# The meta tokens' part of a Mamba-2 scan's states: a product with 16 rows replaced by one with 128

## The chip, the cores and the metric

The kernel runs on one core of a Trainium2 chip. The metric is the device time of one execution in microseconds, lower is better. Three runs of the kernel before took 1002.24, 1003.0 and 1005.76 us; their median, 1003.0 us, is the time before.

TensorE multiplies matrices. An instruction pair does it: a weight load puts a stationary operand (rows x columns) into the array, and a matmul streams a moving operand through it and writes PSUM. The rows are the dimension that is summed over. A float32 product is issued as two passes, so two loads and two matmuls. A transpose is a product of a tile with the identity. VectorE (DVE in the profile), ScalarE (ACT) and GpSimd (POOL) do the rest; SyncE (SP) and GpSimd issue most of the DMAs.

## The reference, cut to what matters

A layer of a hybrid decoder: 512 tokens with 16 learned meta tokens ahead of them, so 528 positions, 1024 channels. One of its branches is a Mamba-2 scan with 32 heads of 64 channels in 8 groups of 4 heads, in chunks of 128 positions. The sequence is padded in front, so that the 16 meta tokens are a chunk of their own. The part that the change touches is the states of the chunks:

```python
a_cs = jnp.cumsum(a_dt, axis=2)
...
decay_states = jnp.exp(a_cs[:, :, -1:] - a_cs)
states = jnp.einsum("bclgn,bclgr,bclgrp->bcgrpn", bf, decay_states, xdt)
```

For each chunk c and group g this is a sum over the chunk's positions l of B (128 state channels n) times x (4 heads x 64 channels), weighted per position and head by dt (it is in xdt = x * dt) and by the decay to the end of the chunk. For the meta tokens' chunk the sum has 16 terms, for the three later chunks whose states are needed 128.

## The kernel before, in words

Everything stands with channels on the partitions and positions in the free dimension. `group_proj` computes for one group the projections and the short convolution: `bt` (B, 128 x 528), `ct` (C, 128 x 512), `xc` (x, two tiles of 128 x 528) and `zt`. Positions 0 to 15 of `bt` and `xc` are the meta tokens; `tok(c)` selects the 128 positions of chunk c behind them. `ssd` does the group's scan. Both are generators: `weave` interleaves the scan of group g with the projections of group g + 1 (in the last group with `out_part`, and in group 4 with `out_half` too). The order on each engine is planned ahead from these; pools give the tiles, and an instruction waits for the last reader of the space that its tile takes.

Before the first group, `dt_out` turns dt and its sums to position-major form: `dtok` and `dtm` (16 x 2 x 32: dt and the cumulated a*dt of the meta tokens), and from them the decays `dec` (for the chunks) and `decm` (16 x 32, for the meta tokens). It runs while the gates' projections (`gate_pool`) and the normalization of u (`norm_u`) go on.

In `ssd`, the first step transposes B and x, so that positions stand on the partitions. Three chunks of B and the 16 meta positions go into one PSUM bank, `ptb` (lines 473 to 475); two ScalarE copies take them to `btok` (128 x 3 x 128, line 476) and `btm` (16 x 128, line 477). The meta positions of x go to `ptm` (line 480) and from there, times dt, to `xdtm` (16 x 256, VectorE, line 481). The four chunks of x go to `ptx` and, times dt, to `xdt` (lines 488 and 489). Two more VectorE multiplies apply the decays: `xddm` from `xdtm` (line 494) and `xdd` from `xdt` (line 495). Lines 499 to 513 make the decay matrix in `abc`.

The second step multiplies C with B into `pcb` (line 522), and then makes the four states in two PSUM banks `pst`: the meta tokens' with 16 rows (line 529), the three chunks' with 128 rows (line 531). In every group the eight loads and matmuls of `pcb`, the two of line 529 and the six of line 531 follow each other directly on TensorE. A ScalarE copy (line 533) takes the first state, and VectorE accumulates the others (lines 538 and 539). The third step makes the outputs `po` and `py` from the states and from `abc` (lines 550 and 556); later steps normalize them to `yh` and `yl` (lines 581 to 585), which `out_half` (products `pso`) and `out_part` (`psp`) read as float32r pairs of a high and a low part.

The scan's tiles come from the pool `gs`, whose space is used by others after the scan: among these the 16 T tiles (`t13h` to `t42l`, line 889), which GpSimd's queue loads in order from device memory.

Of the kernel before, what the change touches and what calls it, by code (L numbers as in the profile page):

```python
# [9 lines left out]
F32 = mybir.dt.float32  # L10
F32R = mybir.dt.float32r
AF = mybir.ActivationFunctionType
ALU = mybir.AluOpType

P = 128
D = 1024
SEQ = 512
NM = 16
# [4 lines left out]
R = 4  # L23
HEADS = 32
# [39 lines left out]
def kernel(ctx: ExitStack, tc, xT, x, w, f1, f2, vec, fnw, out):  # L64
    nc = tc.nc
    act, dve, pe, pool = nc.scalar, nc.vector, nc.tensor, nc.gpsimd

    const = ctx.enter_context(tc.tile_pool(name="const", bufs=1, side="left"))
# [64 lines left out]
    ident = const.tile([P, P], F32, name="ident")  # L133
# [20 lines left out]
    dtm = const.tile([NM, 2, HEADS], F32, name="dtm")  # L154
    dec = const.tile([P, 4, HEADS], F32, name="dec")
    cdec = const.tile([P, 4, HEADS], F32, name="cdec")
    decm = const.tile([NM, HEADS], F32, name="decm")

    u_stack = ExitStack()
    up = u_stack.enter_context(tc.tile_pool(name="up", bufs=1, side="left"))  # L160
# [12 lines left out]
    def psum1(name):  # L173
        return psb.tile([P, 512], F32, tag="s", name=name)
# [40 lines left out]
    H = HEADS  # L215
# [105 lines left out]
    for t, name in ((rsh, "dgh"), (rsl, "dgl")):  # L321
        d = pre.tile([NT, 6, NT], F32R, tag="sq", name=name, bufs=2)
# [3 lines left out]
    for i in range(2):  # L326
        pb = psum1(f"pb1_{i}")
        c = slice(3 * i, 3 * i + 3)
        for n in range(2):
            pe.matmul(pb[:, : 3 * NT], ones_r[:NT], dg[n][:, c, :].rearrange("p a b -> p (a b)"),  # L330
                      start=n == 0, stop=n == 1)
# [11 lines left out]
    for c in range(4):  # L343
        r = slice(c * H, (c + 1) * H)
# [19 lines left out]
    for c in (slice(0, P), slice(P, W)):  # L364
        n = c.stop - c.start
# [4 lines left out]
    def dt_out():  # L370

        pt = psum1("pt_dt")
        for j, src in enumerate((dt, acs)):
            pe.transpose(pt[:, j * P : (j + 1) * P], src[:, :P], ident)
            pe.transpose(pt[:NM, 256 + j * H : 256 + (j + 1) * H], src[:H, P:], ident[:H, :H])
        dve.tensor_copy(dtok.rearrange("p a c h -> p (a c h)"), pt[:, :256])
        dve.tensor_copy(dtm.rearrange("p a h -> p (a h)"), pt[:NM, 256 : 256 + 2 * H])
        pq = psum1("pq_dt")
        pe.matmul(pq[:, :128], sel[:, 0, :], dtok[:, 1, :, :].rearrange("p c h -> p (c h)"),
                  start=True, stop=True)  # L380
        pe.matmul(pq[:NM, 128 : 128 + H], sel[:NM, 1, :NM], dtm[:, 1, :], start=True, stop=True)
        fl = lambda t: t.rearrange("p c h -> p (c h)")
        dve.tensor_tensor(fl(dec), pq[:, :128], fl(dtok[:, 1, :, :]), op=ALU.subtract)
        dve.tensor_tensor(decm, pq[:NM, 128 : 128 + H], dtm[:, 1, :], op=ALU.subtract)
        act.activation(fl(dec), fl(dec), AF.Exp)
        act.activation(decm, decm, AF.Exp)
        act.activation(fl(cdec), pq[:, :128], AF.Exp)


# [65 lines left out]
    def bc(ap, n):  # L455
        return ap.unsqueeze(len(ap.shape)).to_broadcast(list(ap.shape) + [n])

    def ssd(g, cur):

        xc, bt, ct, zt = cur  # L460
        hs = slice(R * g, R * g + R)
        tok = lambda c: slice(NM + c * P, NM + (c + 1) * P)
        ctok = lambda c: slice(c * P, (c + 1) * P)
        flat = lambda t: t.rearrange("p r d -> p (r d)")
# [1 line left out]
        abc_load[g] = nc.gpsimd.dma_start(abc, acs_d[hs, :].partition_broadcast(P))  # L466

        xdt = gs.tile([P, 4, R, 64], F32, tag="xdt", name=f"xdt{g}")
        xdtm = gs.tile([NM, R, 64], F32, tag="xdtm", name=f"xdtm{g}")
        btok = gs.tile([P, 3, P], F32, tag="btok", name=f"btok{g}")  # L470
        btm = gs.tile([NM, P], F32, tag="btm", name=f"btm{g}")
        ptb = psum1(f"ptb{g}")
        for c in range(3):
            pe.transpose(ptb[:, c * P : (c + 1) * P], bt[:, tok(c)], ident)
        pe.transpose(ptb[:NM, 3 * P :], bt[:, :NM], ident)
        act.copy(btok.rearrange("p c n -> p (c n)"), ptb[:, : 3 * P])
        b_meta[g] = act.copy(btm, ptb[:NM, 3 * P :])
        pm = psum1(f"ptm{g}")
        for i in range(2):
            pe.transpose(pm[:NM, i * P : (i + 1) * P], xc[:, i, :NM], ident)  # L480
        dve.tensor_tensor(xdtm, pm[:NM, :256].rearrange("p (r d) -> p r d", r=R),
                          bc(dtm[:, 0, hs], 64), op=ALU.mult)
        for b in range(2):
            pt = psum1(f"ptx{g}_{b}")
            for c in range(2):
# [4 lines left out]
                              pt.rearrange("p (c r d) -> p c r d", c=2, r=R),  # L490
                              bc(dtok[:, 0, 2 * b : 2 * b + 2, hs], 64), op=ALU.mult)
        xdd = gs.tile([P, 3, R, 64], F32, tag="xdd", name=f"xdd{g}")
        xddm = gs.tile([NM, R, 64], F32, tag="xddm", name=f"xddm{g}")
        dve.tensor_tensor(xddm, xdtm, bc(decm[:, hs], 64), op=ALU.mult)
        x_decayed[g] = dve.tensor_tensor(xdd, xdt[:, :3, :, :], bc(dec[:, :3, hs], 64), op=ALU.mult)

        eb = gs.tile([P, 2, SEQ], F32, tag="eb", name=f"eb{g}")
# [28 lines left out]
        st = [gs.tile([P, R, 64], F32, tag=f"st{c}", name=f"st{c}_{g}") for c in range(4)]  # L526
        pss = [psum1(f"pst{g}_{b}") for b in range(2)]
        pv = [pss[c // 2][:, (c % 2) * 256 : (c % 2) * 256 + 256] for c in range(4)]
        pe.matmul(pv[0], btm, flat(xddm), start=True, stop=True)
        for c in range(3):  # L530
            pe.matmul(pv[c + 1], btok[:, c, :], xdd[:, c, :, :].rearrange("p r d -> p (r d)"),
                      start=True, stop=True)
# [7 lines left out]
        for rs_ in ((slice(0, 2), slice(2, R)) if g == G - 1 else (slice(0, R),)):  # L540
            n = rs_.stop - rs_.start
            masked[g] = dve.tensor_tensor(dm[:, rs_], dm[:, rs_], cbm.unsqueeze(1).to_broadcast([P, n, 4, P]),
                                          op=ALU.mult)
# [3 lines left out]
        for i in range(2):  # L547
# [5 lines left out]
            for c in range(4):  # L553
                for j in range(2):
                    r = 2 * i + j
# [33 lines left out]
    done, abc_load, masked, y_first, squared, b_meta, x_decayed = {}, {}, {}, {}, {}, {}, {}  # L589
# [22 lines left out]
    for d in range(GATES_FIRST):  # L612
        gate_pool(d, True)
        if d == 0:
            dt_out()
# [3 lines left out]
    gs = gc_stack.enter_context(tc.tile_pool(name="gs", bufs=1, side="left", reuse_waits="tile"))  # L619
# [137 lines left out]
    for g in range(G):  # L757
        nxt = group_tiles(g + 1) if g + 1 < G else None
        fill = [group_proj(g + 1, nxt, GATE_AT.get(g))] if nxt else [out_part()]
        if g == 4:  # L760
            fill = [out_half()] + fill
        if g in SUMS_AT:
            fill.append(sums_of_u(SUMS_AT.index(g), g))
        if g in SETS_AT:
            fill.append(weight_sums_at(g))
        weave(ssd(g, cur), fill, 2 if g == 4 else 1)
        cur = nxt
# [633 lines left out]
    for c in range(NC - 1):  # L1401
        z, e = c == 0, c == NC - 2

        n = 2 * c + 3
# [63 lines left out]
    c = NC - 1  # L1468
# [14 lines left out]
    for t in range(4):  # L1483
        T, st = t // 2, slice((t % 2) * P, (t % 2 + 1) * P)
        n = 0
        for half in range(2):
            parts = [(0, 512)] if half == 0 or t < 3 else [(0, 256), (256, 256)]
            for a, m in parts:
# [3 lines left out]
                i = 0  # L1492
# [4 lines left out]
                for k, seg in ((1, (A11, 3)[T]), (0, (A12, A22)[T])):  # L1497
                    wh, wl = wq[k, half]
                    for p in range(2):
                        x0 = p * 512 + a  # L1500
                        f = i == 0 and not (T == 0 and half == 0) and not a
                        i += 1
                        for lhs, rhs in ((hh, wh), (hh, wl), (hl, wh)):
                            pe.matmul(ps, lhs[:, p, seg, st], rhs[:, x0 : x0 + m], start=f and lhs is hh and rhs is wh,
                                      stop=i == 4 and lhs is hl, skip_group_check=True)
# [150 lines left out]
```

## Time and profile before

| | us |
|---|---|
| median of three runs | 1003.0 |
| lowest and highest run | 1002.24, 1005.76 |
| span of the profiled execution | 1001.4 |
| scan of the eight groups, in the profiled execution | 70 to 460 |

The profile is one execution on the chip, taken by the hardware profiler; its own time is its span, 1001.4 us from the first to the last instruction, 1.6 below the median of the runs. Engines: PE is TensorE's matmuls, PEld its weight loads, which overlap the matmuls. A group's line reads: line of the kernel, engine, operation, output<-inputs, shape of output and input, how often | busy time in us, mean ns of one | idle time of the engine just before them, and what ended most of it. "issue" is idle time for which the profile names no other engine. In the timeline a row begins with its start and its duration in us, and rows of equal instructions that follow each other are merged with a count (x3); a shape such as 16*128 is rows times columns of the stationary operand. In the chain of waits, a row is the time that an instruction added to the chain that ended last. Ends of matmuls are modelled.

### The profile page before, as it was taken

Reading aid. Unit: us, or ns where it says so; the run is one execution under the profiler, and the core shown is the slowest. Engines: PE = TensorE matmul, PEld = TensorE weight load, DVE = VectorE, ACT = ScalarE, POOL = GpSimd, SP = SyncE. Lnnn points to the kernel's source line nnn. Section 1 sums busy time; section 2 is a strip of 40 time slices with the busy share of each in tenths; the row PEclk is TensorE's granted clock in tenths of the full one; section 3 lists DMA queues with packets and bytes.
Section 4 is the critical chain, followed back from the end, with each engine's and each line's share of the span. In section 5 each row is a group of like instructions: output and inputs, shape, how many; then the busy total and the mean of one; then the engine's idle time right before and its main releaser. Section 6 shows DMA issues by size and latency. Waiting matters only on the chain.

```text
span 1001.4 us, 15539 instructions
## 1 busy us (share of the span) xinstructions
PE 993.2 (99%) x6095; PEld 878.3 (88%) x6095; DVE 793.2 (79%) x1147; ACT 602.8 (60%) x840; POOL 88.1 (9%) x148
## 2 busy tenths in 40 slices
PE   9999999999999999999999999999999999999997
PEld 7889898999889998988998888888889999999986
DVE  7988797979736687979789667876988888888885
ACT  8675958595827439483255343368666656656654
POOL 0022101111002011002201001121100000000000
PEclk9999999999999999999999999999999999999999
DMA  7378763678238635417978632879654464454432
GB/s 242 92 281 226 202 185 117 193 188 234 63 104 253 164 99 160 132 38 213 280 203 234 230 105 71 238 194 303 182 189 148 149 189 149 146 187 150 127 105 85
DMA packets 56202, 171.47 MB, mean 171 GB/s; under 512 B 6400, under 2 KB 7744, under 8 KB 55104
## 3 DMA queue, kind: packets, MB, share of 16 engines
q1 hardware_dynamic: 36576, 105.86, 32.5%
q0 software_dynamic: 18832, 63.71, 24.3%
q8 instruction: 48, 0.79, 0.3%
q10 hardware_dynamic: 720, 0.91, 0.3%
q14 instruction: 26, 0.21, 0.1%
HBM read 161.90 MB, written 48.40 MB: 210 GB/s over the span
## 4 chain that ended last, share of the span: by engine, by line
PE 98%; DMA 1%; ACT 0%; DVE 0%; issue 0%; SPq 0%; ACTq 0%
PE px L191 12%; PE px L1291 8%; PE alpha L1359 6%; PE pz L191 6%; PE px L193 6%; PE px L1294 4%; PE alpha L1362 3%; PE pgp L191 3%; PE pz L193 3%; PE pgs L191 3%; PE py L556 2%; PE pso L127 2%; PE po L550 2%; PE wo_alpha L1053 1%; PE pso L128 1%; PE pso L130 1%
## 5 line engine op out<-in xcount | busy, mean ns | idle before, releaser
L93 ACT CAST whi<-raw 128x1024 fp32r<-128x1024 f32 (+2 forms) x98 | 98.5, 1014 | 105.7 <-PE px L193 33.2
L95 DVE TENSOR_TENSOR wlo<-raw,whi 128x1024 fp32r<-128x1024 f32 (+2 forms) x98 | 114.7, 1176 | 50.9 <-ACT whi L93 33.1
L191 PE MATMUL px<-uh,whi 128*128 128x264 f32 (+1 forms) x448 | 113.2, 291 | 0.0
L193 PE MATMUL px<-ul,whi 128*128 128x264 f32 (+1 forms) x448 | 110.5, 285 | 0.0
L191 PEld LDWEIGHTS px<-uh,whi 128*128 128x128 f32 x448 | 84.6, 189 | 1.8 <-issue 1.4
L193 PEld LDWEIGHTS px<-ul,whi 128*128 128x128 f32 x448 | 84.3, 188 | 0.4 <-issue 0.2
L1066 DVE TENSOR_TENSOR ht<-ht,alpha 128x1024 f32<-128x1024 f32 x35 | 42.7, 1219 | 29.1 <-PE alpha L1359 29.1
L989 ACT CAST shi<-rawf 128x1024 fp32r<-128x1024 f32 x42 | 44.2, 1051 | 28.7 <-PE alpha L1362 18.2
L191 PE MATMUL px<-uh,wlo 128*128 128x264 f32 (+1 forms) x448 | 58.5, 283 | 0.0
L191 PEld LDWEIGHTS px<-uh,wlo 128*128 128x128 f32 x448 | 55.9, 188 | 0.0
L1359 PE MATMUL alpha<-shi,hh 128*128 128x512 f32 x140 | 55.2, 394 | 0.0
L1362 PE MATMUL alpha<-shi,hl 128*128 128x512 f32 x140 | 54.7, 391 | 0.0
L990 DVE TENSOR_TENSOR slo<-rawf,shi 128x1024 fp32r<-128x1024 f32 x42 | 51.2, 1218 | 0.6 <-ACT shi L989 0.6
L1294 PE MATMUL px<-vsl,shi 128*128 128x256 f32 x192 | 47.4, 280 | 0.0
L1291 PE MATMUL px<-vsh,shi 128*128 128x256 f32 x192 | 47.4, 281 | 0.0
L193 PE MATMUL pz<-ul,whi 128*128 128x512 f32 x112 | 43.6, 390 | 0.0
L191 PE MATMUL pz<-uh,whi 128*128 128x512 f32 x112 | 43.6, 389 | 0.0
L577 DVE RECIPROCAL rs<-rs 128x128 f32<-128x128 f32 x32 | 27.2, 909 | 13.9 <-ACT rs L575 13.8
L1359 PE MATMUL alpha<-slo,hh 128*128 128x512 f32 x140 | 37.4, 389 | 0.0
L1291 PEld LDWEIGHTS px<-vsh,shi 128*128 128x128 f32 x192 | 36.2, 188 | 0.9
L1294 PEld LDWEIGHTS px<-vsl,shi 128*128 128x128 f32 x192 | 36.1, 188 | 0.9
L1294 PE MATMUL px<-vl,shi 128*128 128x256 f32 x144 | 36.1, 283 | 0.0
(558 smaller groups left out, 2859.1 us busy)
## 6 DMA issues: line engine op xcount, KB each, us to landing
raw<-in_w SPq DMA_DIRECT2D x104, 512.0 KB, 4.4
f_t<-in_f POOLq DMA_DIRECT2D x38, 512.0 KB, 6.7
f_s<-in_f POOLq DMA_DIRECT2D x26, 512.0 KB, 8.6
b<-in_f SPq DMA_DIRECT2D x21, 512.0 KB, 4.6
rawf<-in_f SPq DMA_DIRECT2D x36, 256.0 KB, 3.2
rawf<-f_t SPq DMA_DIRECT2D x36, 256.0 KB, 3.0
abc<-acs_d POOLq DMA_DIRECT2D x8, 1024.0 KB, 7.6
f_t<-f_t POOLq DMA_DIRECT2D x12, 512.0 KB, 4.4
```

The costliest lines, as they stand in the source:

```text
L93: act.copy(hi[:, c], raw[:, c])
L95: dve.tensor_tensor(lo[:, c], raw[:, c], hi[:, c].bitcast(F32), op=ALU.subtract)
L191: pe.matmul(o, wt, rhs[0][k][:, c], start=part == 0 and k == 0, stop=part == 1 and k == NK - 1)
L193: pe.matmul(o, wt, rhs[1][k][:, c], start=False, stop=False)
L577: dve.reciprocal(rs[:, ctok(c)], rs[:, ctok(c)])
L989: splits.append((act.copy(hi, src), dve.tensor_tensor(lo, src, hi.bitcast(F32), op=ALU.subtract)))
L990: dve.tensor_tensor(lo, src, hi.bitcast(F32), op=ALU.subtract)))
L1066: added[0] = dve.tensor_tensor(o, o, src, op=op)
L1291: pe.matmul(ps, m, f[k][0], start=start and not low and k == 0, stop=stop and low == 1 and k == 3, skip_group_check=True)
L1294: pe.matmul(ps, m, f[k][1], start=False, stop=False, skip_group_check=True)
L1359: pe.matmul(ps[t], hh[:, p, seg, st], m, start=bool(first and not low and p == 0), stop=bool(last and low and p == 1), skip_group_check=True)
L1362: pe.matmul(ps[t], hl[:, p, seg, st], m, start=False, stop=False, skip_group_check=True)
```

## The change

The meta tokens' chunk is treated as a whole chunk of 128 positions: positions 0 to 127, of which the first 16 are the meta tokens. The 112 others get weight zero.

- `wmeta` (128 x 32) takes the place of `decm` (16 x 32). It is set to zero once at the start. `dt_out` writes its first 16 rows: the decay, as before, and then times dt (one multiply more, once).
- The transposes of lines 475 and 480 take positions 0 to 127 instead of 0 to 15: 8 + 16 transposes with 128 stationary columns instead of 16.
- `btok` has four parts and is copied by one ScalarE instruction of 512 columns; `btm` and its copy are gone.
- `xddm` (128 x 256) is made by one VectorE multiply with `wmeta`, from PSUM; `xdtm` and its multiply are gone.
- The first state's product has 128 rows. Rows 16 to 127 add zeros, so the state is the same sum.

A partition's share of the pool `gs` becomes 1 KB smaller (`xdtm` 1 KB and `btm` 0.5 KB go, `btok` grows by 0.5 KB), so the tiles behind lie at other places. The later lines of the changed kernel have numbers that are lower by up to two.

```diff
-    decm = const.tile([NM, HEADS], F32, name="decm")
+    wmeta = const.tile([P, HEADS], F32, name="wmeta")
+    dve.memset(wmeta, 0.0)
...
-        dve.tensor_tensor(decm, pq[:NM, 128 : 128 + H], dtm[:, 1, :], op=ALU.subtract)
+        dve.tensor_tensor(wmeta[:NM], pq[:NM, 128 : 128 + H], dtm[:, 1, :], op=ALU.subtract)
         act.activation(fl(dec), fl(dec), AF.Exp)
-        act.activation(decm, decm, AF.Exp)
+        act.activation(wmeta[:NM], wmeta[:NM], AF.Exp)
+        dve.tensor_tensor(wmeta[:NM], wmeta[:NM], dtm[:, 0, :], op=ALU.mult)
         act.activation(fl(cdec), pq[:, :128], AF.Exp)
...
-        xdtm = gs.tile([NM, R, 64], F32, tag="xdtm", name=f"xdtm{g}")
-        btok = gs.tile([P, 3, P], F32, tag="btok", name=f"btok{g}")
-        btm = gs.tile([NM, P], F32, tag="btm", name=f"btm{g}")
+        btok = gs.tile([P, 4, P], F32, tag="btok", name=f"btok{g}")
+        xddm = gs.tile([P, R, 64], F32, tag="xddm", name=f"xddm{g}")
         ptb = psum1(f"ptb{g}")
         for c in range(3):
             pe.transpose(ptb[:, c * P : (c + 1) * P], bt[:, tok(c)], ident)
-        pe.transpose(ptb[:NM, 3 * P :], bt[:, :NM], ident)
-        act.copy(btok.rearrange("p c n -> p (c n)"), ptb[:, : 3 * P])
-        b_meta[g] = act.copy(btm, ptb[:NM, 3 * P :])
+        pe.transpose(ptb[:, 3 * P :], bt[:, :P], ident)
+        b_meta[g] = act.copy(btok.rearrange("p c n -> p (c n)"), ptb)
         pm = psum1(f"ptm{g}")
         for i in range(2):
-            pe.transpose(pm[:NM, i * P : (i + 1) * P], xc[:, i, :NM], ident)
-        dve.tensor_tensor(xdtm, pm[:NM, :256].rearrange("p (r d) -> p r d", r=R),
-                          bc(dtm[:, 0, hs], 64), op=ALU.mult)
+            pe.transpose(pm[:, i * P : (i + 1) * P], xc[:, i, :P], ident)
+        dve.tensor_tensor(xddm, pm[:, :256].rearrange("p (r d) -> p r d", r=R),
+                          bc(wmeta[:, hs], 64), op=ALU.mult)
...
-        xddm = gs.tile([NM, R, 64], F32, tag="xddm", name=f"xddm{g}")
-        dve.tensor_tensor(xddm, xdtm, bc(decm[:, hs], 64), op=ALU.mult)
...
-        pe.matmul(pv[0], btm, flat(xddm), start=True, stop=True)
+        pe.matmul(pv[0], btok[:, 3, :], flat(xddm), start=True, stop=True)
```

## The prediction

> **What bounds the kernel now.** I read the head of the page first (span, busy times, chain), then the busy times by stage, then the chain around one of the products that the change rewrites, then TensorE's weight loads there one by one.
>
> ```profile
> span 1001.4 us, 15539 instructions
> PE 993.2 (99%) x6095; PEld 878.3 (88%) x6095; DVE 793.2 (79%) x1147; ACT 602.8 (60%) x840; POOL 88.1 (9%) x148
> ...
> PE 98%; DMA 1%; ACT 0%; DVE 0%; issue 0%; SPq 0%; ACTq 0%
> ```
>
> The chain that ends last runs on TensorE for 98% of the span. VectorE (DVE) and ScalarE (ACT) have spare time. So an edit counts where it takes time out of TensorE's own stream, or makes TensorE wait. The next view gives the stages, and shows which engine is full in each.
>
> ```profile
> core 0: us, PE busy (x) PEld busy (x) DVE busy (x) ACT busy (x) POOL busy (x), PEclk, DMA share, GB/s
> 0.00:70.00 70.00, 67.85 (x426) 58.03 (x427) 59.26 (x109) 50.36 (x75) 9.06 (x22) 1.00 0.59 192
> 70.00:460.00 390.00, 389.98 (x2649) 350.39 (x2648) 299.65 (x470) 255.64 (x342) 43.19 (x70) 1.00 0.56 161
> 460.00:640.00 180.00, 180.00 (x958) 155.89 (x956) 136.19 (x190) 74.19 (x101) 21.67 (x35) 1.00 0.66 200
> 640.00:1001.00 361.00, 355.42 (x2067) 314.00 (x2065) 298.14 (x380) 222.59 (x322) 14.17 (x21) 1.00 0.55 164
> ```
>
> The scan of the eight groups, where the change sits, runs from 70 to 460 us. TensorE is busy in all of it, at the full granted clock. "Busy" is modelled, though: a matmul that is held up is only drawn longer. The chain shows more, because it splits the same stretch by who used it. This is group 0's piece:
>
> ```profile
> 76.54 0.89 PE pcb L522 x8
> 77.43 0.62 PE pst L529 x2
> 78.06 1.49 PE pst L531 x6
> 79.55 0.12 PE px L191
> ```
>
> All eight instructions of pst have 256 columns (a float32 product is issued as two passes). The two with 16 rows (L529) cost 0.31 us each, the six with 128 rows (L531) 0.25 us. The weight loads of the same moment show why:
>
> ```profile
> 76.82 0.42 PEld L522 LDWEIGHTS pcb<-ct,bt 128*128 128x128 f32 x3
> 77.36 0.29 PEld L529 LDWEIGHTS pst<-xddm,btm 16*128 16x128 f32 x2
> 77.98 1.16 PEld L531 LDWEIGHTS pst<-xdd,btok 128*128 128x128 f32 x6 [0.33 <-issue]
> 79.17 0.19 PEld L191 LDWEIGHTS px<-uh,whi 128*128 128x128 f32 x1
> ...
> 78.52 0.62 PEld L531 LDWEIGHTS pst<-xdd,btok 128*128 128x128 f32 x3
> ```
>
> Loads normally follow each other at the pace of the matmuls. The three pcb loads step by (0.42 - 0.19)/2 = 0.115 us, the last three pst loads by (0.62 - 0.19)/2 = 0.215 us. The last pcb load is at 76.82 + 0.23 = 77.05, so the next is due at 77.165; it comes at 77.36. Behind the 16-row pair the load engine sits idle for 0.33 us, and the profile names no other engine ("issue"). So TensorE empties when it goes from 128 rows to 16, and again on the way back.
>
> **The change part by part. The product with 128 rows** (L529). If nothing empties, the first pst load is at 77.165, the second 0.115 later (behind pcb's last matmul), and the next six steps and the one to px take 0.215 each: 77.165 + 0.115 + 7 x 0.215 = 78.785, against 79.17 now. That is 0.385 us, and the chain says the same: 0.62 + 1.49 - 8 x 0.215 = 0.39. The view by line says that this repeats:
>
> ```profile
> L531 PEld LDWEIGHTS pst<-xdd,btok 128*128 128x128 f32 x48 | 8.5, 189 | 3.5 <-issue 2.3 <-DVE wlo L95 0.3
> L529 PEld LDWEIGHTS pst<-xddm,btm 16*128 16x128 f32 x16 | 2.3, 183 | 1.0
> ```
>
> Sixteen loads of L529 are eight groups, and 2.3 + 0.3 us is eight times 0.33. So 8 x 0.385 = 3.1 us go. Bounds: no saving at all if the emptying has another cause; 3.1 if every pair behaves as here. That rows are the cause is supported by a second place, in dt_out, where 128 and 32 rows alternate:
>
> ```profile
> 51.01 0.14 PEld L374 LDWEIGHTS pt_dt<-ident,ddt 128*128 128x128 f32 x1
> 51.43 0.08 PEld L375 LDWEIGHTS pt_dt<-ident,ddt 32*16 32x16 f32 x1 [0.29 <-issue]
> ```
>
> Again an idle 0.29 us named "issue" where the row count falls. I take 3.1.
>
> Two rules bear on it. The Trainium skill, TensorE: Matmul & The Clock Gate (Step-by-step: what each phase is for), says that a weight load's time goes with its columns and that its row count does not matter; the loads agree (183 ns with 16 rows, 189 with 128), and by that alone the product would save nothing. The Trainium skill, TensorEngine Tiling (Array Packing) (Key Properties), says that changing the tiling mode drains the engine; the idle 0.33 us agrees, and by it the saving is the one above.
>
> **Wider transposes** (L475, L480): 8 + 16 of them go from 16 to 128 stationary columns.
>
> ```profile
> 69.25 0.09 PEld L475 LDWEIGHTS ptb<-ident,bt 128*16 128x16 f32 x1
> 69.36 0.20 PEld L480 LDWEIGHTS ptm<-ident,xc 128*16 128x16 f32 x2
> 69.57 0.91 PEld L488 LDWEIGHTS ptx<-ident,xc 128*128 128x128 f32 x8
> ```
>
> A 16-column load lasts 0.09 us. The 128-column ones last about 0.14 (the L374 row), but both start 0.11 us apart (69.25 to 69.36 to 69.57 by three; (0.91 - 0.14)/7 for the eight). The cover is the matmul of the neighbour, which streams the same 128 columns of ident either way. Cost 0; without that cover 24 x 0.05 = 1.2 us, the upper bound.
>
> **VectorE and ScalarE.** Per group one VectorE multiply goes (xddm from xdtm), the other now covers 128 partitions; on ScalarE two copies become one of 512 columns.
>
> ```profile
> L539 DVE TENSOR_TENSOR st<-st,pst 128x256 f32<-128x256 f32 x24 | 9.9, 411 | 0.1
> L481 DVE TENSOR_TENSOR xdtm<-ptm,dtm 16x256 f32<-16x256 f32 x8 | 3.3, 406 | 2.9 <-PE ptm L480 2.9
> L494 DVE TENSOR_TENSOR xddm<-xdtm,decm 16x256 f32<-16x256 f32 x8 | 3.2, 403 | 0.0
> L384 DVE TENSOR_TENSOR decm<-pq_dt,dtm 16x32 f32<-16x32 f32 x1 | 0.2, 169 | 0.0
> ...
> L476 ACT COPY btok<-ptb 128x384 f32<-128x384 f32 x8 | 3.8, 475 | 0.0
> L533 ACT COPY st<-pst 128x256 f32<-128x256 f32 x8 | 2.9, 363 | 1.4 <-PE pst L531 1.4
> L477 ACT COPY btm<-ptb 16x128 f32<-16x128 f32 x8 | 2.0, 250 | 0.0
> ```
>
> On VectorE, 256 columns cost 406 ns on 16 partitions and 411 on 128, so the surviving multiply costs the same, and 8 x 0.403 = 3.2 us go. The new product in dt_out costs one 0.17 us, and the memset under 0.1. On ScalarE, 128 columns more cost 475 - 363 = 112 ns, so a 512-column copy takes some 587 ns (an estimate from these two rows), and 8 x (475 + 250 - 587) = 1.1 us go. None of this is on the chain: I count 0, and keep 0.40 + 0.14 us per group as the bound of a gain. The new product waits for ScalarE's exp, with norm_u's work queued behind it; it lies some 12 us ahead of the scan, at worst 0.2 us.
>
> **Moved instructions.** The planned order of the two kernels differs little. What matters is group 4: on VectorE one slice of L509 and xdd now stand ahead of the pair yl (L585), and TensorE's first pcb stands inside the pso burst.
>
> ```profile
> 260.43 1.27 DVE L489 TENSOR_TENSOR xdt<-ptx,dtok 128x512 f32<-128x512 f32 x2
> 261.63 0.40 DVE L494 TENSOR_TENSOR xddm<-xdtm,decm 16x256 f32<-16x256 f32 x1
> 262.46 1.29 DVE L585 TENSOR_TENSOR yl<-yt,yh 128x512 fp32r<-128x512 f32 x2 [0.43 <-ACT yh L584]
> 263.67 0.95 DVE L495 TENSOR_TENSOR xdd<-xdt,dec 128x768 f32<-128x768 f32 x1
> 264.54 0.67 DVE L509 TENSOR_SCALAR abc<-abc,dtok 128x128 f32<-128x128 f32 x3
> ...
> 263.81 0.19 PEld L128 LDWEIGHTS pso<-yl,whi 128*128 128x128 f32 x1 [0.21 <-DVE yl L585]
> ```
>
> After xdt (261.70) come 0.22 us of L509 and 0.95 of xdd, then yl until 262.87 + 1.29 = 264.16 instead of 263.75. TensorE already waits 0.21 us for the second yl; it would wait 0.4 longer, less the 0.115 of a pcb pass done early: +0.3 us (bounds 0 and 0.4). Behind it on TensorE stand the rest of pso and pst, all in order. In groups 2 and 3 xdd also moves forward, but there no pso burst reads yl at that time.
>
> The T tiles that POOL loads after the scan get their waits at other places, because the scan's tiles lie 1 KB lower. This is their queue and their first use:
>
> ```profile
> 475.46 2.12 POOL L889 DMA_DIRECT2D t42l<-t_d42l  x4
> ...
> DMA to landing us min/median/max: 7.1/8.3/8.7
> ...
> 509.98 0.28 PE L843 MATMUL pxx<-t42h,whiS 128*128 128x260 f32 x1
> ```
>
> The last one is issued at 477.0, lands some 8.7 us later at 486, and is read from 510: 24 us of room, so 0.
>
> **Sum**: 1001.4 - 3.1 + 0 + 0.3 = 998.6 us for the profiled execution. The median of the timed runs, 1003.0, lies 1.6 above that execution's span, so 1003.0 - 2.8 = 1000.2 us. Nothing later takes it back by these rows: from 460 to 640 us TensorE is busy throughout, at 0.66 DMA share.
>
> **The rivals.** *More than the emptying.* If the 0.54 us per group freed on VectorE and ScalarE also shortened a wait of TensorE in each group, 8 x 0.54 = 4.3 us more would go: 995.9. For it: TensorE's loads do wait for VectorE here and there (the 0.21 us above). Against it: VectorE and ScalarE have 0% of the chain.
>
> *Not what it says.* The emptying stays, because something else between pcb and pst makes it (a change of bank or of operands): 1003.0 + 0.3 = 1003.3. For it: the row count leaves the load's duration alone. Against it: the idle time behind the pair and the second place in dt_out. The rule of the Trainium skill on row counts (TensorE: Matmul & The Clock Gate, the section named above) gives this by itself.
>
> *Slower.* The T tiles come too late. POOL issues in order; if an early load now waits for the last reader of a scan tile late in the out_part stretch, all sixteen queue behind it. It decides from 24 us of delay on; at 32 us TensorE would stand for 8 us: 1000.2 + 8 = 1008.2. For it: the waits do move to earlier loads. Against it: the same readers have finished by 475 in the trace, and the issue of sixteen loads takes only 16 x 0.53 = 8.5 us.
>
> **How the numbers follow.** Half a per cent, 5.0 us, is about what a measurement can tell from no change, so faster means under 998.0 and slower over 1008.0. Chances: the forecast 0.62, more than the emptying 0.22, not what it says 0.08, the slower rival 0.08. The forecast alone spans 999 to 1001.5: 0 to 1.2 us of transposes and 0 to 0.4 in group 4 on one side, some of the freed time on the other. The range that leaves out the far half of the second case, most of the third and all of the fourth is 995.5 to 1003.0. Faster: 0.22 and 0.05 from the lower edge of the forecast, 0.27. Slower: 0.08. Within: 0.65.
>
> **What would show it.** Right: no "issue" idle of about 0.33 us ahead of the pst loads, the eight passes from pcb's last load to px in 1.62 us instead of 2.0, the transposes still 0.11 us apart, and a span of about 998.6. Wrong: the idle time stays, or it goes and the span keeps its length (then a wait took its place, in group 4's pso first), or the span shrinks by over 5 us (then VectorE or ScalarE had held TensorE after all).

## The result, and the profile after

| | before | after |
|---|---|---|
| median of 22 runs each, us | 1003.2 | 1001.38 |
| lowest and highest run, us | 1002.24, 1005.76 | 1000.4, 1004.98 |
| span of the profiled execution, us | 1001.4 | 999.8 |

The ratio of the times is 0.9982, with a 95% interval of 0.9976 to 0.9988. So the change saves 1.8 us: a gain that can be told from nothing, but inside the half per cent that the prediction called no change. The forecast was a saving of 2.8 us, to 1000.2, and a span of 998.6 us for the profiled execution; it came to 999.8.

The head of the profile after, and the first line of its chain of waits:

```profile
span 999.8 us, 15519 instructions
PE 991.7 (99%) x6095; PEld 879.2 (88%) x6095; DVE 790.8 (79%) x1141; ACT 602.6 (60%) x832; POOL 88.3 (9%) x148
...
PE 96%; ACT 2%; DMA 0%; issue 0%; DVE 0%; SPq 0%; ACTq 0%
```

TensorE still sets the end, and executes as many instructions as before. ScalarE now has 2% of the chain. Next, TensorE's weight loads in group 0's scan after the change (start, duration, instruction), then the two groups of pst by line:

```profile
76.07 0.98 PEld L520 LDWEIGHTS pcb<-ct,bt 128*128 128x128 f32 x8
76.97 0.30 PEld L527 LDWEIGHTS pst<-xddm,btok 128*128 128x128 f32 x2
77.30 1.27 PEld L529 LDWEIGHTS pst<-xdd,btok 128*128 128x128 f32 x6
78.59 0.19 PEld L192 LDWEIGHTS px<-uh,whi 128*128 128x128 f32 x1
```

```profile
L529 PEld LDWEIGHTS pst<-xdd,btok 128*128 128x128 f32 x48 | 9.1, 190 | 1.2
L527 PEld LDWEIGHTS pst<-xddm,btok 128*128 128x128 f32 x16 | 2.4, 192 | 0.0
```

The idle 0.33 us named "issue" is gone in all groups: of the 3.5 us of idle time ahead of the three-chunk loads 1.2 are left, and none ahead of the meta tokens' pair; what is left is named by no wait. From the first pst load to px it takes 78.59 - 76.97 = 1.62 us. Before, the pair was due at 77.165 and px came at 79.17: 2.005.

To see where a gain goes, one can match the matmuls of two traces in their order, and take the difference of the start times of the same matmul. Where this difference (after less before) jumps, time was won or lost. In after it jumps by -0.387 us at the pst pair of every group, so 8 x 0.387 = 3.10 us were won there. But from 70 to 460 us, over the whole scan, the difference falls by only 2.05 us, and ahead of and behind the scan it moves by -0.19 and +0.58. The experiments look for the missing 1.05 and 0.58.

### The profile page after: what moved, and what is told of

It reads as the page before. It is cut to its first block, busy times and chain, and to the rows that moved or that the text cites. A ratio compares the mean times of both kernels' runs of the same rounds, so it can differ in the third digit from the quotient of the medians.

```text
span 999.8 us, 15519 instructions
## 1 busy us (share of the span) xinstructions
PE 991.7 (99%) x6095; PEld 879.2 (88%) x6095; DVE 790.8 (79%) x1141; ACT 602.6 (60%) x832; POOL 88.3 (9%) x148
## 4 chain that ended last, share of the span: by engine, by line
PE 96%; ACT 2%; DMA 0%; issue 0%; DVE 0%; SPq 0%; ACTq 0%
PE px L192 12%; PE px L1289 8%; PE alpha L1357 6%; PE px L194 6%; PE pz L192 5%; PE px L1292 4%; PE alpha L1360 3%; PE pgs L192 3%; PE pgp L192 3%; PE pz L194 3%; PE py L554 2%; PE po L548 2%; PE pf L128 1%; PE pf L127 1%; PE wo_alpha L1051 1%; PE pgp L194 1%
```

## The experiments

Each kernel is the changed one with the edit shown. Unless said otherwise, its time and ratio are against runs of the kernel before on the same chip at the same time. Four numbers come up for all of them, so they stand together here: the change of TensorE's start times against the trace of before (us, negative is a gain) over the first four groups (70 to 240 us), group 4 with what runs beside it (240 to 310), the last three groups (310 to 460), and the rest (460 to 990). Ahead of the scan, from 0 to 70 us, the executions differ from before's by -0.70 (rows16) to +0.71 us (rows64), all of it in the first 30 us but for 0.13 us in dt_rows and g4_dt; this is left out.

| kernel | median | ratio, 95% interval | 70-240 | 240-310 | 310-460 | rest |
|---|---|---|---|---|---|---|
| after | 1001.38 | 0.9982, 0.9976-0.9988 | -1.09 | -0.01 | -0.94 | +0.58 |
| again | 1001.66 | 0.9989, 0.9980-0.9999 | -1.07 | +0.65 | -0.96 | +0.07 |
| rows16 | 1003.18 | 0.9999, 0.9990-1.0007 | -0.01 | +0.06 | +0.03 | +0.65 |
| rows64 | 1003.89 | 1.0002, 0.9993-1.0010 | +0.12 | +0.05 | -0.20 | +0.44 |
| rows72 | 1000.98 | 0.9975, 0.9965-0.9984 | -1.20 | +0.13 | -1.03 | +0.07 |
| g4_order | 1001.54 | 0.9983, 0.9974-0.9992 | -1.10 | +0.04 | -0.95 | +0.03 |
| dt_rows | 1001.66 | 0.9987, 0.9978-0.9996 | -1.08 | 0.00 | -0.96 | +0.07 |
| g4_dt | 1001.68 | 0.9984, 0.9976-0.9993 | -1.08 | +0.23 | -0.55 | +1.70 |
| g4_acc | 1001.40 | 0.9980, 0.9971-0.9989 | -1.08 | -0.07 | -0.89 | +0.45 |
| g4_dve | 1001.43 | 0.9976, 0.9966-0.9986 | -1.08 | +0.01 | -0.93 | +0.01 |
| rows72_dve | 1000.92 | 0.9974, 0.9965-0.9983 | -1.19 | -0.01 | -1.01 | +0.01 |

By the emptying alone the three stretches of the scan would read -1.55, -0.39 and -1.16.

### How many rows it takes

```diff
-        pe.matmul(pv[0], btok[:, 3, :], flat(xddm), start=True, stop=True)
+        pe.matmul(pv[0], btok[:16, 3, :], flat(xddm)[:16], start=True, stop=True)
```

This is rows16; rows64 and rows72 have 64 and 72 in both places. All else in the change stays: the wide transposes, one copy, one multiply.

> The changed kernel with the first 16 rows alone given to the meta tokens' product (the rows behind are zero, so the sum is the same); wide transposes, one copy of 512 columns, one multiply and the order of all engines stay as in the changed kernel. Theory (the array empties where the row count changes): the idle 0.33 us named issue is back behind the pair in all eight groups, the eight pst passes take 0.387 us longer each time, span 999.8 + 3.1 = 1002.9, so about 1.0011 of the time before. Rival (the gain came from the freed VectorE and ScalarE time): span stays near 999.8, ratio near 0.998. Wide transposes cost 0 if the loads stay 0.11 us apart.

> As rows16, with 64 rows in the product. If the array empties because it goes to a form with fewer row strips (32 or 64) and back, 64 rows cost as much as 16: idle 0.33 us per group, span near 1002.9, ratio about 1.001. If only the smallest form (up to 32 rows) does it, 64 rows are as good as 128: span 999.8, ratio 0.998. If the cost grows with the rows left out, about half: span 1001.3.

> As rows16, with 72 rows in the product. If the forms are 32, 64 and 128 rows, 72 rows run in the form of 128: no idle time behind the pair, span 999.8, ratio 0.998. If any row count other than the neighbour's empties the array: idle 0.33 us per group, span near 1002.9, ratio 1.001. The sums with 88 rows in the prologue (L330) follow their neighbours at the usual 0.12 us in the profile before, which speaks for the first.

The loads of pst by line, first of rows16, then of rows64, then of rows72:

```profile
L529 PEld LDWEIGHTS pst<-xdd,btok 128*128 128x128 f32 x48 | 8.5, 189 | 3.5 <-issue 2.3 <-DVE wlo L95 0.3
L527 PEld LDWEIGHTS pst<-xddm,btok 16*128 16x128 f32 x16 | 2.3, 182 | 1.0
```

```profile
L529 PEld LDWEIGHTS pst<-xdd,btok 128*128 128x128 f32 x48 | 8.5, 189 | 3.5 <-issue 2.3 <-DVE wlo L95 0.3
L527 PEld LDWEIGHTS pst<-xddm,btok 64*128 64x128 f32 x16 | 2.4, 184 | 1.0
```

```profile
L529 PEld LDWEIGHTS pst<-xdd,btok 128*128 128x128 f32 x48 | 9.1, 189 | 1.3
L527 PEld LDWEIGHTS pst<-xddm,btok 72*128 72x128 f32 x16 | 2.4, 191 | 0.0
```

With 16 and with 64 rows the idle time is that of before, to the tenth; with 72 it is that of after. So the rows alone make it, and the step lies between 64 and 72 rows. The time follows: rows16 and rows64 take what the kernel before takes, rows72 what after takes or a little less. The Trainium skill, TensorEngine Tiling (Array Packing) (Tiling Modes), has row tilings of 32 and 64 rows and none between 64 and 128, and its Key Properties say that a change of mode drains the engine; these three runs agree with both, and 0.387 us is what going there and back costs here. The mode itself is not in the traces; they show the idle time.

rows16 also prices the rest of the change. Its scan differs from before's by -0.01 + 0.06 + 0.03 = +0.08 us: the wide transposes, and the multiply and the copy that VectorE and ScalarE no longer do, together change nothing that shows. That a small cost of the ones hides a small gain of the others is not excluded by this sum.

### The same kernel again

No edit: the changed kernel, profiled a second time.

> The changed kernel once more, unaltered. Shift of TensorE's instructions against the profile before: -2.0 us over the scan (70 to 460) if the loss of about 1 us there (group 4 and the pace of the products behind pst) is the program's; nearer -2.8 if it was chance. At the start of the MLP (675 to 685) the first profile lost 0.5 us more behind a late weight load: if that is the program's it is there again, if chance the shift stays the same there, as it did with 72 rows.

Over the scan this execution wins 1.07 - 0.65 + 0.96 = 1.38 us, not the 2.0 expected, so of the loss in the scan only a part repeats. The rest behind the scan loses 0.07 us here and 0.58 in the first profile of the same program. These are the loads that waited in the first one, and then the only one that waited at the same place in the second:

```profile
678.57 0.19 PEld L127 LDWEIGHTS pf<-vh,whi 128*128 128x128 f32 x1 [0.32 <-ACT vh L1092]
679.09 0.19 PEld L128 LDWEIGHTS pf<-vl,whi 128*128 128x128 f32 x1 [0.33 <-DVE vl L1093]
```

```profile
678.82 0.19 PEld L128 LDWEIGHTS pf<-vl,whi 128*128 128x128 f32 x1 [0.16 <-DVE vl L1093]
```

So this loss is one execution's, not the change's. Six of the eleven executions lose less than 0.1 us behind the scan and five lose 0.4 to 1.7, rows16 among them. A span of one execution therefore can't settle half a microsecond; the four columns can, where they repeat. 70 to 240 us repeats to 0.03 us over all seven executions with 128 rows. In 240 to 310 the second profile lost 0.66 us more than the first: 0.34 of it ahead of 260 us, and 0.33 at VectorE's yl in group 4; these are that execution's own.

### Group 4

Three edits aim at the stretch of group 4, where nearly all of that group's 0.387 us, or more, is lost in every run without the emptying. In g4_order VectorE's xdd waits for the last yl, as it did before the change (the lines that note the last yl are left out):

```diff
-        x_decayed[g] = dve.tensor_tensor(xdd, xdt[:, :3, :, :], bc(dec[:, :3, hs], 64), op=ALU.mult)
+        with tc.issue_after(y_low[3].ins) if g == 4 else nullcontext():
+            x_decayed[g] = dve.tensor_tensor(xdd, xdt[:, :3, :, :], bc(dec[:, :3, hs], 64), op=ALU.mult)
```

> The changed kernel with xdd of group 4 put behind group 3's yl pair on VectorE, as the kernel before had it; TensorE's first pcb then stands behind the pso burst again. Theory (the moved xdd costs 0.3 us in group 4): the loss in group 4 goes, scan 0.3 us shorter than again, span about 0.3 us below again. Rival (the loss there comes from the pso bank's copy, which follows the pace of TensorE): no change.

This was a miss. yl came first again (261.25 us, xdd at 262.47), but the stretch reads +0.04, and -0.01 in after: nothing was won. The reason stands in the next two views: TensorE's loads around pst in group 4, and ScalarE at that time, both of after.

```profile
261.89 0.41 PEld L520 LDWEIGHTS pcb<-ct,bt 128*128 128x128 f32 x2
...
262.75 0.19 PEld L128 LDWEIGHTS pso<-yl,whi 128*128 128x128 f32 x1 [0.23 <-DVE yl L583]
...
265.47 0.30 PEld L527 LDWEIGHTS pst<-xddm,btok 128*128 128x128 f32 x2
265.80 1.27 PEld L529 LDWEIGHTS pst<-xdd,btok 128*128 128x128 f32 x6
267.51 0.19 PEld L127 LDWEIGHTS pso<-yh,whi 128*128 128x128 f32 x1 [0.45 <-ACT acc L636]
```

```profile
262.64 1.04 ACT L93 CAST whi<-raw 128x1024 fp32r<-128x1024 f32 x1
263.69 1.28 ACT L510 ACT_TABLE_LOAD   x1
264.99 1.06 ACT L510 ACTIVATE abc<-abc 128x1024 f32<-128x1024 f32 x1
265.95 1.04 ACT L511 ACTIVATE abc<-abc 128x1024 f32<-128x1024 f32 x1
266.90 0.56 ACT L636 COPY acc<-pso 128x512 f32<-128x512 f32 x1
```

The wait for yl is 0.23 us, hardly more than the 0.21 of before. TensorE reads that yl 0.23 us later against before, but two passes of pcb now stand ahead of it, which it would else do behind the burst; with them taken into account nothing is lost at yl in this execution. The loss comes behind pst: the next pso load needs the PSUM bank that ScalarE's copy acc empties, and that copy stands behind a table load and two exps. It ends at 267.46, and the load starts at 267.51. The same copy and the same load in the kernel before:

```profile
268.22 0.57 ACT L638 COPY acc<-pso 128x512 f32<-128x512 f32 x1
268.84 0.19 PEld L127 LDWEIGHTS pso<-yh,whi 128*128 128x128 f32 x1
```

The copy ended at 268.79, when TensorE had just finished its loads of pst, so that no wait is named. Now TensorE gets there earlier, and waits for the copy: of the 0.387 us, 0.31 go back at this load. In g4_order the same load waits as long:

```profile
267.60 0.19 PEld L127 LDWEIGHTS pso<-yh,whi 128*128 128x128 f32 x1 [0.43 <-ACT acc L637]
```

g4_acc therefore puts the exps behind ScalarE's copy of the first state, as the last group has it; the planner then moves three pst products behind a pso burst:

```diff
-        if g < G - 1:
+        if g < G - 1 and g != 4:
             done[g] = decay()
...
-        if g == G - 1:
+        if g in (4, G - 1):
             with tc.issue_after(st0.ins):
                 decay()
```

> The changed kernel, but in group 4 ScalarE's two exps of the decay matrix (L512, L513) stand behind its copy of the first state, as they do already in the last group, so that ScalarE's copy of the pso bank (acc) comes ahead of them; on TensorE the last three products of pst then stand ahead of one more pso burst or behind it, as the planned order has it. Theory (in group 4 what was given back is TensorE's wait of 0.45 us for the acc copy, because ScalarE had the exps in front of it): the named wait for acc behind pst goes, the shift of TensorE between 260 and 272 us becomes about -0.35 to -0.45 against before, the span is 0.3 us shorter (about 999.0 to 999.5), ratio about 0.998. Rival: the masked multiply on VectorE and the products py of group 4 now come later than the exps did before, TensorE waits there instead, and the span is the same or up to 2 us longer. Other rival: the loads still wait at that place, for another engine (VectorE's yl), and nothing changes.

Loads, then ScalarE, of g4_acc:

```profile
266.18 0.19 PEld L127 LDWEIGHTS pso<-yh,whi 128*128 128x128 f32 x1 [0.32 <-ACT acc L636]
```

```profile
262.71 2.94 ACT L93 CAST whi<-raw 128x1024 fp32r<-128x1024 f32 x3
265.54 0.59 ACT L636 COPY acc<-pso 128x512 f32<-128x512 f32 x1
```

Three casts of weight blocks took the place of the exps; the copy ends at 266.13 and the load starts at 266.18. The theory's place was right and its remedy wrong: in both orders ScalarE has something ahead of the copy. g4_dve gives this one copy to VectorE:

```diff
-                act.copy(acc[2 * dd + i], ps[:, i * SEQ : (i + 1) * SEQ])
+                (dve.tensor_copy if 2 * dd + i == 0 else act.copy)(acc[2 * dd + i], ps[:, i * SEQ : (i + 1) * SEQ])
```

> The changed kernel, but the first of the eight copies acc<-pso (L636) is done by VectorE, which idles 0.85 us in group 4 before its multiply cbm (265.78 in the trace of the changed kernel); all else is as planned from that, which puts the three later products of pst behind one pso burst. Theory (the wait of 0.45 us behind pst in group 4 is for that copy alone, which ScalarE starts late whatever stands in front of it): the loads of pso no longer wait there, TensorE's shift against before goes down by the full 0.35 to 0.45 in group 4, the scan's change is -2.35 to -2.5 us instead of -2.05, span about 999.3, ratio 0.9975 to 0.998. Rival: VectorE's copy stands behind a weight block's low part (1.2 us) or delays cbm and the masked multiply, a wait of the same 0.3 to 0.45 us for VectorE takes its place, and the group keeps its net of -0.1.

> As g4_dve, and the product of the meta tokens with 72 rows. Theory: 72 rows cost what 128 cost, so the time is that of g4_dve within 0.5 us (about 1000.9 to 1001.3, ratio 0.997 to 0.998); if both small gains are real it is the fastest of the versions tried. Rival: the lower time of rows72 was the scatter of its executions, and this one stands at the changed kernel's 1001.4.

The loads of g4_dve, and VectorE's copy:

```profile
262.78 0.19 PEld L128 LDWEIGHTS pso<-yl,whi 128*128 128x128 f32 x1 [0.19 <-DVE yl L583]
262.89 0.19 PEld L127 LDWEIGHTS pso<-yh,whi 128*128 128x128 f32 x1
263.38 0.19 PEld L128 LDWEIGHTS pso<-yl,whi 128*128 128x128 f32 x1 [0.30 <-DVE yl L583]
...
266.12 0.30 PEld L527 LDWEIGHTS pst<-xddm,btok 128*128 128x128 f32 x2
266.51 0.19 PEld L127 LDWEIGHTS pso<-yh,whi 128*128 128x128 f32 x1
```

```profile
265.77 0.69 DVE L636 COPY acc<-pso 128x512 f32<-128x512 f32 x1 [0.20 <-PE pso L130]
```

Now no wait is left behind pst, and from 264.3 to 275 us TensorE wins 0.60 us against before, where after wins 0.31: the 0.3 us are back. (Both figures, and the losses that follow, hold the 0.23 us of the two pcb passes, which stand ahead of the yl load in these kernels.) But this execution lost 0.58 at the yl loads (0.19 and 0.30 us of waiting) where after lost 0.23, and the stretch again ends at 0. In rows72_dve it is the same: 0.55 won behind pst, 0.47 lost at yl. The loss at yl is not this edit's alone: the two profiles of the unaltered kernel lost 0.23 and 0.56 there, which is 0 and 0.33 without the pcb passes. That VectorE reaches yl at its own pace, so that TensorE can lose there what it gained before, is argued from this and not shown. So the cause behind pst is shown, and the net of the edit is not told apart from zero.

### The same emptying in dt_out

dt_rows takes the emptying out of the second place that the prediction showed. The small transposes of dt, and the small product, get 128 rows (dtm has 128 partitions then, zero behind the 16th):

```diff
-            pe.transpose(pt[:NM, 256 + j * H : 256 + (j + 1) * H], src[:H, P:], ident[:H, :H])
+            pe.transpose(pt[:NM, 256 + j * P : 256 + (j + 1) * P], src[:, P:], ident)
...
-        pe.matmul(pq[:NM, 128 : 128 + H], sel[:NM, 1, :NM], dtm[:, 1, :], start=True, stop=True)
+        pe.matmul(pq[:NM, 128 : 128 + H], sel[:, 1, :NM], dtm[:, 1, :], start=True, stop=True)
```

> The changed kernel with dt_out's small products in 128 rows too: two transposes with 32 rows and one product with 16 rows (rows of zeros behind, dtm 128 rows). Theory (the array empties between up to 64 rows and more): the idle 0.29 us before L375 goes, the four transposes take 0.45 us instead of 0.93 to the next load and the two products 0.25 less: TensorE is 0.6 us earlier from 54 us on than in again. Rival (only pst's case empties, for its bank or its operands): no idle time goes; the wider transposes cost 0.1 us.

> Both edits, g4_order and dt_rows, together. Theory: 0.9 us below again, ratio to the kernel before about 0.9965 to 0.997, the fastest of all. Rival: what is gained at 54 us is lost in waits before the scan ends, ratio as again.

The loads of dt_out in dt_rows:

```profile
50.78 0.14 PEld L376 LDWEIGHTS pt_dt<-ident,ddt 128*128 128x128 f32 x1
51.01 0.09 PEld L377 LDWEIGHTS pt_dt<-ident,ddt 128*16 128x16 f32 x1
51.12 0.14 PEld L376 LDWEIGHTS pt_dt<-ident,dacs 128*128 128x128 f32 x1
51.22 0.09 PEld L377 LDWEIGHTS pt_dt<-ident,dacs 128*16 128x16 f32 x1
51.33 0.19 PEld L193 LDWEIGHTS pgp<-xh,whi 128*128 128x128 f32 x1
...
52.77 0.30 PEld L381 LDWEIGHTS pq_dt<-dtok,sel 128*128 128x128 f32 x2 [0.44 <-DVE dtok L378]
```

The idle 0.29 us is gone: the four transposes take 51.33 - 50.78 = 0.55 us, where before they took 51.94 - 51.01 = 0.93. But the sums' product then waits 0.44 us for VectorE's copy dtok. From 49 to 58 us the kernel gains 0.13 us, neither the 0.38 of the transposes nor the 0.6 expected, and its time is not told apart from after's. g4_dt joins this edit and g4_order's. It gains the same 0.13 us there. Its execution lost 0.39 us at 329.6 and 1.7 behind the scan, and its median of 1001.68 is no better than that of either edit.

### A pace that the row count sets

What remains of the missing 1.05 us? Group 4 holds 0.38 (0.39 less the 0.01 of its stretch). A second part is in the products px directly behind pst in group 0: 32 of them lie between the two rows of the chain of waits of each kernel, first after, then rows72, then rows16:

```profile
78.97 0.12 PE px L192
...
82.81 1.93 PE px L192 x16
```

```profile
78.77 0.12 PE px L192
...
82.55 1.93 PE px L192 x16
```

```profile
78.85 0.12 PE px L192
...
82.60 1.94 PE px L192 x16
```

They take 3.84 us in after, 3.78 in rows72 and 3.75 in rows16, as in the kernel before (from the row at 79.55, shown with the prediction, to the same row at 83.30): 120, 118 and 117 ns each, of the same shape, at the same granted clock. This repeats. In groups 0, 2 and 6, 28 of these products came on average 119.9 to 120.0 ns apart in all seven executions with 128 rows, 118.1 apart in both with 72, 118.5 in rows64, and 116.8 in before and rows16; in groups 1, 3 and 5 it was 118.5, 116.8, 119.1 and 118.3. The pace is slowed with the emptying (64 rows) and without it (128), and it does not rise steadily with the rows. Against before, 0.09 us in each of three groups, 0.27 in all, goes back in this way with 128 rows. Why the pace of later products hangs on the row count of an earlier one stays open.

Most of the last 0.4 us is in three steps that stand at the same places in after and again, and not in rows16: 0.07 us at po in group 1, 0.18 us at po in group 3, and 0.1 us at 444 us in group 7. The trace tells of the one in group 3. These are six passes of po and the VectorE addition whose result the fifth and sixth read, in before and in after:

```profile
225.92 0.41 DVE L539 TENSOR_TENSOR st<-st,pst 128x256 f32<-128x256 f32 x1
226.19 0.83 PE L550 MATMUL po<-ct,st 128*128 128x128 f32 x6
```

```profile
224.74 1.01 PE L548 MATMUL po<-ct,st 128*128 128x128 f32 x6
224.79 0.41 DVE L537 TENSOR_TENSOR st<-st,pst 128x256 f32<-128x256 f32 x1
```

The passes come 0.11 us apart, so the fifth is due 0.44 us behind the first. In before the addition ends at 226.33, 0.14 us behind the first; in after at 225.20, 0.46 us behind it, and the six take 1.01 us instead of 0.83. No run moves this addition, so that it is the cause is read from the times and not tested. The other steps weren't pursued.

The two executions with 72 rows gain 1.19 and 1.20 us from 70 to 240, those with 128 rows 1.07 to 1.10. It is a steady 0.1 us, in the direction of the medians (1000.98 and 1000.92 against 1001.38), but the intervals of the ratios overlap, so that 72 rows are faster than 128 in time isn't shown.

## Why the prediction was right, and where it was off

- *The product with 128 rows, -3.1 us.* Right in place, cause and size: -0.387 us in each of eight groups, 1.62 us for the eight passes, no idle time left. rows16 and rows64 bring the idle time back, rows72 doesn't. The rival that something else between pcb and pst empties the array falls with them.
- *Wider transposes, 0.* Right: 8 + 16 wide transposes in rows16 leave its scan within 0.08 us of before, and in after the loads of group 0 still start 0.11 us apart (L476 at 69.06, two of L480 at 69.17, L488 at 69.38).
- *VectorE and ScalarE off the chain, 0.* Right for what they no longer do: the multiply takes 419 ns on 128 partitions and the 512-column copy 580 ns (411 and 587 were expected), and in rows16, which keeps all of this, the scan is no shorter than before. The rival of 995.9 us falls with it. That both stay off the chain when TensorE gets faster was not right, as the next points show.

```profile
L481 DVE TENSOR_TENSOR xddm<-ptm,wmeta 128x256 f32<-128x256 f32 x8 | 3.4, 419 | 3.1 <-PE ptm L480 3.1
L477 ACT COPY btok<-ptb 128x512 f32<-128x512 f32 x8 | 4.6, 580 | 0.0
```

- *Group 4, +0.3 us by yl standing behind xdd.* The size came near (+0.38), by luck, since the mechanism failed. Against TensorE's products yl came 0.23 us later, not 0.4, and two pcb passes of together 0.23 us, not one of 0.115, filled that time. What went back is 0.31 us behind pst: TensorE came earlier to a bank that ScalarE had not emptied, and waits 0.45 us for the copy there. The other 0.07 us goes between 277 and 310 us, nearly as in rows16 (0.05). A loss at yl did come in some executions (0.33 us in again, none in after), with xdd ahead of it or not.
- *The T tiles, 0.* Right; the last load is issued by 475.3 us in after, before its old time of 477.0, so the slower rival did not come.

```profile
473.19 2.12 POOL L887 DMA_DIRECT2D t42l<-t_d42l  x4
```

- *"Nothing later takes it back."* This step failed. The sum of the terms was -2.8; the scan gave -2.05 in the profile, and the median fell by 1.8. Of the 3.10 us that the emptying gave, 0.38 went back in group 4, 0.27 by the slower pace of px, 0.18 at po in group 3, and some 0.2 in smaller steps, all inside the scan. The sentence was argued from TensorE being busy from 460 to 640 us, which says nothing on the scan or on the pace of TensorE's own instructions; and the 0% of VectorE and ScalarE in the chain told of the old order only, in which acc's copy and the addition of group 3 were done in time with 0.05 and 0.30 us to spare. In the profiled execution 0.58 more went behind the scan, but that is chance, since the same program loses 0.07 in its second profile.
- *The range.* The median of 1001.38 lies at the upper edge of the forecast's own 999 to 1001.5. The costs that this edge was made of, wide transposes and yl, are not what was paid in the profile, so that it lies inside is in part luck.

## What to carry to other kernels

When products with 128 rows stand around one with 64 or fewer on TensorE, it is worth padding the small one with zero rows to over 64: here 72 and 128 rows cost TensorE's stream nothing, and the gain was 0.39 us a time around pst. To find such places, look for idle time named "issue" ahead of a load where the row count changes; the name alone isn't enough, since g4_dt's trace has 0.32 us of it at 329.31 between two loads of the same shape. Such a gain counts in full only until TensorE's next wait for another engine: ask at each place where it reads or reuses what VectorE or ScalarE delivers whether it was early enough before (acc behind pst in group 4, and dtok in dt_out, were not). And with gains of a microsecond, profile the same program twice before explaining a difference: here 0.5 us of one trace was chance.

## What the runs showed of the hardware that was not expected

- The step lies between 64 and 72 rows: 64 rows cost as much idle time as 16 (2.3 us in seven groups, named "issue", and 0.3 in the eighth), and 72 none. The row counts between weren't tried.
- A weight load's duration says nothing of it: 182, 184, 191 and 192 ns with 16, 64, 72 and 128 rows.
- 258-column products run at 116.8 to 120.0 ns each at the same granted clock, for about 30 of them in a row, and which it is depends on the row count of the product ahead of them and on the group, reproducibly.
- A change of columns shows idle time of the same name in some places: in before 0.35 to 0.36 us ahead of py's loads with 64 columns three times (at 286.41, 299.50 and 447.30) and 0.17 us on the way back (at 287.43), but none between the transposes with 16 and 128 columns. No run changed these, so the cause isn't shown.
